# One sum-and-transpose step for four modulation blocks in a four-layer diffusion trunk

## The chip, the cores and the metric

One core of a Trainium2 chip runs the whole program in one launch. The metric is the device time of that launch in microseconds (us); of the kernel before, three timed runs are shown. The five engines are named as the profile names them: PE is TensorE's matmul side and PEld its weight loads, DVE is VectorE, ACT is ScalarE, POOL is GpSimd, SP issues transfers.

## The reference, cut to what matters

Four layers (mixers HGRN2, neighbourhood attention, S5, HGRN2) work on 256 context and 256 latent tokens of width 1024. Each layer has six modulation vectors for the latents and six for the context, made by one large product of two vectors with a matrix of 1024 x 6144:

```
s_lat, s_ctx = jax.nn.silu(c), jax.nn.silu(c_ctx)
for i in range(DEPTH):
    m_l = jnp.split((s_lat @ w_mod[i] + b_mod[i])[:, None, :], N_MOD, axis=-1)
    m_c = jnp.split((s_ctx @ w_mod[i] + b_mod[i])[None, None, :], N_MOD, axis=-1)
    h_l = rmsnorm(lat, norm_g[i, 0]) * (1.0 + m_l[1]) + m_l[0]
    h_c = rmsnorm(cx, norm_g[i, 0]) * (1.0 + m_c[1]) + m_c[0]
    ...
    lat = lat + m_l[2] * rmsnorm(y_l, norm_g[i, 1])
    h_l = rmsnorm(lat, norm_g[i, 2]) * (1.0 + m_l[4]) + m_l[3]
    lat = lat + m_l[5] * rmsnorm(conv_ffn(h_l, ...), norm_g[i, 3])
```

The context stream does the same with `m_c`. The change touches only how `s @ w_mod` is formed and brought into place.

## The kernel before, in words

Activations lie with features on the partitions and tokens along the row. Every large product is done as three single-pass products (high part by high part, low by high, high by low: lines 691 to 693), over 8 slices of the feature axis; ACT and POOL or DVE split the weights into high and low parts (lines 112 and 115) one weight tile ahead. The order of the work is the order in which the program text issues it: each engine runs its instructions in that order, and generators that are advanced at "ticks" put small work between the products. The program runs a mixer and a feed-forward part (FFN) for each layer in turn: HGRN2, FFN, attention, FFN, S5, FFN, HGRN2, FFN.

**Modulation blocks.** `w_mod` is cut into 96 blocks, one for each layer `l`, vector `s` (6) and quarter `b` (4): 1024 rows by 256 columns. `mod_load` (line 293) brings one in by two transfers; there is room for one block ahead after the start. Blocks are formed at slots (`mod_slot`, line 406), which `mod_plan` spreads over a mixer or FFN; `mod_until` forms what is still missing before its use. After the start, the slots hold 12 blocks in the first HGRN2, 12 in FFN 0, 12 in attention, 18 in FFN 1, 6 in S5, 15 in FFN 2, 9 in the last HGRN2 and 4 in FFN 3.

**A block on TensorE** (`mod_block`, line 303) is eight matmuls (line 317), each of a 32-column weight tile `sT` (column 0 the context vector, column 1 the latent one, the other 30 zero) against 256 columns of the block, four of them side by side in four column strips of 32. The PSUM tile `ps` then holds four partial sums for each of the two vectors, in rows 32j and 32j+1. ACT copies it to `mev` in SBUF (line 320, one buffer).

**The sum-and-transpose step** (`mod_flush`, line 372) is issued at the next slot: two matmuls (line 386) with a 128x128 half of `mev` as weights and `sel` (128x2, a one in row 32j+c of column c) as the moving side add the four partial sums and turn the 256 features onto the partitions. DVE adds the bias (`mT`, line 390) and, for four of the six vectors, forms the gain `g` (line 398 or 400).

**A block on VectorE** (`mod_vec`, line 328, in FFN 2 alone: `VO = (2,)`) is 16 DVE instructions on 128x256 (lines 336 and 338), one of them after each slice of a product (`vstep`, called from `mm3`); its step is four one-column matmuls (line 383). In FFN 2, 14 blocks are formed so; the 15th is formed on TensorE just before.

Every fp32 matmul of lines 317, 383 and 386 leaves two records in the trace, so a block shows 16 records, a step 4 (line 386) or 8 (line 383).

Of the kernel before, what the change touches and what calls it, by code (L numbers as in the profile page):

```python
# [6 lines left out]
F32 = mybir.dt.float32  # L7
# [8 lines left out]
NK = 8  # L16
# [39 lines left out]
VK = 1  # L56
VO = (2,)
VG = 8
VR = 1
# [13 lines left out]
VEC = {}  # L73
# [81 lines left out]
class Kern:  # L155
    def __init__(self, tc, ctx, a):
# [8 lines left out]
        self.bg = self.vm = None  # L165
        self.von = False
# [87 lines left out]
    def consts(self):  # L254
# [6 lines left out]
        self.sel = cp.tile([128, 2], F32, name="sel")  # L261
# [41 lines left out]
    def mod_block(self):  # L303
# [22 lines left out]
    def mod_vec(self):
        nc = self.nc
        i = self.mod_nd
        r = self.mod_raw[i]
        acc = self.vpool.tile([128, 2, 256], F32, name="mac", bufs=1)  # L330
        for k in range(NK):
            for v in range(2):
                c = self.sT[:, k, v:v + 1]
                w = r[k // 4][:, k % 4]
                if k == 0:
                    nc.vector.tensor_scalar(acc[:, v], w, c, None, op0=MUL)
                else:
                    nc.vector.scalar_tensor_tensor(acc[:, v], w, c, acc[:, v], op0=MUL, op1=ADD)
                if k == 7 and v == 1:
                    self.mod_raw.pop(i)  # L340
                    self.mod_nd += 1
                    self.mod_load()
                    self.mod_flush()
                    self.mod_pend = (i, acc)
                yield
        for _ in range(VG):
            yield
        self.mod_flush()
        for _ in range(VG):
            yield  # L350

    def mod_finish(self):
        g, self.vm = self.vm, None
        for _ in g:
            pass

    def vstep(self):
        if self.vm is None:
            if not self.von:
                return  # L360
            m = self.mod_sched
            if self.mod_nd >= min(m[0] + m[1], self.mod_end):
                return
            self.vm = self.mod_vec()
        for _ in range(VR):
            try:
                next(self.vm)
            except StopIteration:
                self.vm = None
                return  # L370

    def mod_flush(self):
# [5 lines left out]
        l, s, b = self.mod_order[i]  # L378
        ps = self.aux()
        if len(ev.shape) == 3:  # L380
            for c in range(2):
                for v in range(2):
                    nc.tensor.matmul(ps[:, 2 * c + v:2 * c + v + 1], ev[:, v, c * 128:(c + 1) * 128], self.ones,
                                     start=(c == 0 and v == 0), stop=(c == 1 and v == 1), skip_group_check=True)
# [1548 lines left out]
```

## Time and profile before

| what | value |
|---|---|
| timed runs | 2994.34, 2995.45, 2996.59 us (median 2995.45) |
| the profiled execution: span from first to last instruction | 3001.2 us |
| a time of its own for the profiled execution | none is given beside its span |
| busy, share of the span | PE 92%, PEld 76%, DVE 67%, ACT 43%, POOL 27% |
| records | 53651 |
| mean granted TensorE clock | 0.960 of 2.4 GHz |

The span of the profiled execution is 5.75 us (0.2%) above the median of the timed runs. The page of the profile gives the busy time of each engine, the chain of work that ended last, and groups of instructions by line with mean duration, idle time before them and what ended it; the timeline gives instructions in order of time with start and duration, merged where they repeat. A matmul's duration includes its way through the array, so that the cost of one in a stream is read from the distance between two starts.

### The profile page before, as it was taken

The numbers are of one execution on the slowest core, as the hardware profiler recorded it, in microseconds if no ns is written. First come the engines' busy times: TensorE is split into PE (matmuls) and PEld (weight loads), VectorE is DVE, ScalarE is ACT, GpSimd is POOL, SyncE is SP. The second block draws the span as 40 slices with busy tenths as digits, with TensorE's granted clock in tenths as the row PEclk, the third lists the DMA queues.
The fourth block names the chain that finished last, engine by engine and source line by source line (L and its number), as shares of the span: only waits on it lengthen the run. The fifth ranks groups of instructions, "written<-read, shape, count | busy, mean of one in ns | idle before, by whom it ended". The sixth has DMA issues, their size and how long they took to land.

```text
span 3001.2 us, 53651 instructions
## 1 busy us (share of the span) xinstructions
PE 2769.3 (92%) x21814; PEld 2283.6 (76%) x21814; DVE 2016.9 (67%) x3979; ACT 1285.0 (43%) x2154; POOL 824.1 (27%) x440
## 2 busy tenths in 40 slices
PE   8999997999999999889999876989999888998998
PEld 5777776877788777777778734878888887776998
DVE  5676767776657555687555675378677777776776
ACT  4333333633344544553333565453333453332644
POOL 1111112243324111234332311332221342222443
PEclk9999998999999999999999988999999989998998
DMA  6222321255424342235553388323433442232543
GB/s 248 91 100 85 114 86 71 94 186 187 160 105 144 113 162 106 102 128 192 198 197 140 129 238 255 139 87 139 147 133 138 153 171 102 99 113 89 186 173 116
DMA packets 127046, 421.28 MB, mean 140 GB/s; under 512 B 36048, under 2 KB 55760, under 8 KB 102096
## 3 DMA queue, kind: packets, MB, share of 16 engines
q1 hardware_dynamic: 118608, 391.64, 37.5%
q0 software_dynamic: 5472, 23.07, 2.2%
q8 instruction: 172, 2.82, 0.4%
q10 hardware_dynamic: 2720, 3.15, 0.3%
q14 instruction: 74, 0.61, 0.1%
HBM read 392.78 MB, written 29.23 MB: 141 GB/s over the span
## 4 chain that ended last, share of the span: by engine, by line
PE 65%; DVE 20%; ACT 6%; issue 4%; DMA 3%; SPq 1%; POOL 1%; DVEq 0%; ACTq 0%; POOLq 0%
PE acc L691 16%; PE acc L692 15%; PE acc L693 15%; DVE wlo L115 3%; ACT whi L112 2%; PE aux L317 2%; PE aux L1106 2%; DVE FB L1077 2%; PE acc L727 1%; PE acc L729 1%; PE acc L728 1%; DVE y L564 1%; DVE u L896 1%; DVE P L1047 1%; PE aux L1146 1%
## 5 line engine op out<-in xcount | busy, mean ns | idle before, releaser
L115 POOL TENSOR_TENSOR wlo<-wraw,whi 128x1024 fp32r<-128x1024 f32 (+5 forms) x248 | 627.8, 2532 | 1738.2 <-ACT whi L112 1634.2
L691 PE MATMUL acc<-h,whi 128*128 128x512 f32 (+1 forms) x2368 | 869.7, 367 | 26.8 <-ACT h L577 15.7
L692 PE MATMUL acc<-h,whi 128*128 128x512 f32 (+1 forms) x2368 | 843.2, 356 | 21.1 <-DVE h L584 16.7
L693 PE MATMUL acc<-h,wlo 128*128 128x512 f32 (+1 forms) x2368 | 838.8, 354 | 6.1 <-POOL wlo L115 4.0
L691 PEld LDWEIGHTS acc<-h,whi 128*128 128x128 f32 x2368 | 459.1, 194 | 96.5 <-ACT h L577 18.8
L115 DVE TENSOR_TENSOR wlo<-wraw,whi 128x1024 fp32r<-128x1024 f32 (+5 forms) x248 | 400.5, 1615 | 184.5 <-ACT whi L112 154.5
L692 PEld LDWEIGHTS acc<-h,whi 128*128 128x128 f32 x2368 | 459.7, 194 | 81.4 <-DVE h L584 24.0
L693 PEld LDWEIGHTS acc<-h,wlo 128*128 128x128 f32 x2368 | 459.6, 194 | 67.0 <-POOL wlo L115 4.6
L112 ACT ACTIVATE whi<-wraw 128x1024 fp32r<-128x1024 f32 (+5 forms) x496 | 479.5, 1014 | 68.5 <-PE acc L692 51.2
L691 PE MATMUL acc<-gh,whi 128*128 128x256 f32 (+1 forms) x872 | 297.7, 341 | 11.2 <-ACT gh L897 11.2
L693 PE MATMUL acc<-gh,wlo 128*128 128x256 f32 (+1 forms) x872 | 289.6, 332 | 3.0 <-POOL wlo L115 3.0
L692 PE MATMUL acc<-gl,whi 128*128 128x256 f32 (+1 forms) x872 | 289.7, 332 | 1.0 <-DVE gl L898 0.7
L886 ACT ACTIVATE u<-acc,vec 128x512 f32<-128x512 f32 (+1 forms) x190 | 127.4, 691 | 215.1 <-PE acc L693 214.6
L1077 DVE TENSOR_TENSOR FB<-FB,P 128x256 f32<-128x256 f32 x384 | 165.4, 473 | 37.9 <-PE aux L1106 35.2
L691 PEld LDWEIGHTS acc<-gh,whi 128*128 128x128 f32 x872 | 167.5, 192 | 28.8 <-ACT gh L897 12.0
L889 DVE SCALAR_TENSOR_TENSOR u<-acc,vec,u 128x510 f32<-128x510 f32 (+1 forms) x190 | 122.0, 642 | 97.6 <-ACT u L886 97.5
L693 PEld LDWEIGHTS acc<-gh,wlo 128*128 128x128 f32 x872 | 167.0, 192 | 19.9 <-POOL wlo L115 3.8
L692 PEld LDWEIGHTS acc<-gl,whi 128*128 128x128 f32 x872 | 167.2, 192 | 17.7 <-DVE gl L898 2.3
L896 DVE TENSOR_TENSOR u<-u,u 128x512 f32<-128x512 f32 (+1 forms) x95 | 107.5, 1131 | 37.5 <-ACT u L895 34.2
L897 ACT ACTIVATE gh<-u 128x512 fp32r<-128x512 f32 (+1 forms) x95 | 52.3, 551 | 179.6 <-DVE u L896 179.6
L890 DVE SCALAR_TENSOR_TENSOR u<-acc,vec,u 128x510 f32<-128x510 f32 (+1 forms) x190 | 123.1, 648 | 6.7
L1106 PEld LDWEIGHTS aux<-FB 128*32 128x32 f32 (+1 forms) x4416 | 58.4, 114 | 82.0 <-DVE FB L1077 37.4
(299 smaller groups left out, 4328.4 us busy)
## 6 DMA issues: line engine op xcount, KB each, us to landing
wm<-in_w_mod SPq DMA_DIRECT2D x192, 512.0 KB, 5.0
wraw<-in_f_w_in SPq DMA_DIRECT2D x89, 1024.0 KB, 4.8
wraw<-in_fo SPq DMA_DIRECT2D x44, 896.0 KB, 4.5
wraw<-in_a_qz SPq DMA_DIRECT2D x18, 1024.0 KB, 4.9
wraw<-in_a_zg SPq DMA_DIRECT2D x18, 1024.0 KB, 4.9
wraw<-in_fo SPq DMA_DIRECT2D x16, 1024.0 KB, 4.9
wraw<-in_a_v SPq DMA_DIRECT2D x15, 1024.0 KB, 4.9
wraw<-in_c_glu SPq DMA_DIRECT2D x12, 1024.0 KB, 4.8
```

Source lines behind the costliest of these rows:

```text
L112: nc.scalar.activation(hi[:, a:b], r[:, a:b], AF.Copy)
L115: e.tensor_tensor(lo[:, a:b], r[:, a:b], hi[:, a:b].bitcast(F32), op=SUB)
L317: nc.tensor.matmul(ps[32 * j:32 * j + 32, :256], self.sT[:, k, :], r[q][:, j, :], start=(q == 0), stop=(q == 1), tile_position=(0, 32 * j))
L691: nc.tensor.matmul(ps, wh[:, k], hh, start=(first and k == 0), stop=False, **kw)
L692: nc.tensor.matmul(ps, wh[:, k], hl, start=False, stop=False, **kw)
L693: nc.tensor.matmul(ps, wl[:, k], hh, start=False, stop=(last and k == nk - 1), **kw)
L886: nc.scalar.activation(u, ps[c], AF.Identity, scale=w(1), bias=self.vec[:, cb0 + ch:cb0 + ch + 1])
L889: nc.vector.scalar_tensor_tensor(u3[:, :, 1:], p3[:, :, :255], w(0), u3[:, :, 1:], op0=MUL, op1=ADD)
L890: nc.vector.scalar_tensor_tensor(u3[:, :, :255], p3[:, :, 1:], w(2), u3[:, :, :255], op0=MUL, op1=ADD)
L896: nc.vector.tensor_tensor(us[1], us[0], us[1], op=MUL)
L1077: nc.vector.tensor_tensor(o, o, p, op=MUL)
L1106: nc.tensor.matmul(o, FB[:, d, 1 - d, c:c + w], r, start=True, stop=True, tile_position=(0, w * q))
```

## The change

Blocks 8 to 95 are taken in groups of four quarters `b` = 0 to 3 of one vector. `sT` has 40 columns, with the two vectors in columns 6 and 7, and a block of quarter `b` takes the 32 columns from 6-2b on: its sums then come out in rows 32j+2b and 32j+2b+1, and the other rows are zero. For b = 0 ACT copies PSUM to `mev` (two buffers now); for b = 1, 2, 3 DVE adds PSUM to `mev` in SBUF. Only after b = 3 there is a step: two matmuls with `sel` of 8 columns, two DVE instructions for `mT` (one for each 128-row half, of 4x2 elements) and one for `g` on 16 elements. The first 8 blocks keep a step each. The VectorE form (`mod_vec`, `vstep`, `mod_finish`, lines 336, 338 and 383) is gone, and FFN 2 forms its blocks at slots as the other FFNs do.

```diff
-VO = (2,)
...
-        self.sel = cp.tile([128, 2], F32, name="sel")
+        self.sel = cp.tile([128, 8], F32, name="sel")
...
-        self.sT = cp.tile([128, NK, 32], F32, name="sT")
+        self.sT = cp.tile([128, NK, 40], F32, name="sT")
...
     def mod_block(self):
...
+        b = self.mod_order[i][2] if i >= 8 else 0
...
-                nc.tensor.matmul(ps[32 * j:32 * j + 32, :256], self.sT[:, k, :], r[q][:, j, :],
+                nc.tensor.matmul(ps[32 * j:32 * j + 32, :256], self.sT[:, k, 6 - 2 * b:38 - 2 * b], r[q][:, j, :],
                                  start=(q == 0), stop=(q == 1), tile_position=(0, 32 * j))
-        ev = self.np_.tile([128, 256], F32, name="mev", bufs=1)
-        nc.scalar.activation(ev, ps[:, :256], AF.Copy)
+        if b == 0:
+            ev = self.np_.tile([128, 256], F32, name="mev", bufs=2)
+            nc.scalar.activation(ev, ps[:, :256], AF.Copy)
+        else:
+            ev = self.mod_ev
+            nc.vector.tensor_tensor(ev, ps[:, :256], ev, op=ADD)
         self.mod_flush()
-        self.mod_pend = (i, ev)
+        self.mod_ev = ev
+        if i < 8 or b == 3:
+            self.mod_pend = (i, ev)
...
     def mod_flush(self):
...
-        for c in range(2 if len(ev.shape) == 2 else 0):
-            nc.tensor.matmul(ps[:, 2 * c:2 * c + 2], ev[:, c * 128:(c + 1) * 128], self.sel, start=(c == 0),
+        w = 2 * nb
+        for c in range(2):
+            nc.tensor.matmul(ps[:, w * c:w * c + w], ev[:, c * 128:(c + 1) * 128], self.sel[:, :w], start=(c == 0),
                              stop=(c == 1), skip_group_check=True)
...
     def mm3(self, ps, w, h, nk, ticks=(), first=True, last=True, shared=False):
...
-            if k % VK == VK - 1:
-                self.vstep()
...
     def ffn(self, l, halves, nxt):
...
-                    if l not in VO:
-                        self.mod_slot()
+                    self.mod_slot()
...
-                        if not last and m % 2 and l not in VO:
+                        if not last and m % 2:
                             self.mod_slot()
```

Counted over the whole program, TensorE has 768 instead of 656 block matmuls, 60 instead of 164 + 56 matmuls of steps, DVE 66 adds to `mev` instead of 224 instructions on `mac`, 60 instead of 96 for `mT` and 19 instead of 64 for `g`, ACT 30 copies to `mev` instead of 82. POOL and SP issue the same instructions; on SP the transfers of `w_mod` stand elsewhere among those of the weights in FFN 2.

Where the instructions stand, first on PE in FFN 1, at the third block of a group, before a product with `w_out`. Before, the block is followed by the step of the block ahead of it:

```order
L1541 MATMUL aux<-ident,W 128x128 x4
L317 MATMUL aux<-wm,sT 32x256 x8
L386 MATMUL aux<-sel,mev 128x2 x2
L691 MATMUL acc<-gh,whi 128x512
L692 MATMUL acc<-gl,whi 128x512
```

And the same place with the change (lines 1487, 310, 643 and 644 are the former 1541, 317, 691 and 692):

```order
L1487 MATMUL aux<-ident,W 128x128 x4
L310 MATMUL aux<-wm,sT 32x256 x8
L643 MATMUL acc<-gh,whi 128x512
L644 MATMUL acc<-gl,whi 128x512
```

The two matmuls of the step are gone from this slot; they stand, with 8 columns, at the first slot of the next group.

Second, DVE in FFN 2. Before, two pairs of products (`u` is the convolution, `gl` the low part of its result):

```order
L400 TENSOR_TENSOR g_98<-mT,vec 128x4
L889 SCALAR_TENSOR_TENSOR u_19358<-acc,vec,u_19358 128x2x255
L890 SCALAR_TENSOR_TENSOR u_19358<-acc,vec,u_19358 128x2x255
L889 SCALAR_TENSOR_TENSOR u_19362<-acc,vec,u_19362 128x2x255
L890 SCALAR_TENSOR_TENSOR u_19362<-acc,vec,u_19362 128x2x255
L336 TENSOR_SCALAR mac<-wm,sT 128x256 x2
L338 SCALAR_TENSOR_TENSOR mac<-wm,sT,mac 128x256 x3
L896 TENSOR_TENSOR u_19362<-u_19358,u_19362 128x512
L898 TENSOR_TENSOR gl<-u_19362,gh 128x512
L115 TENSOR_TENSOR wlo<-wraw,whi 128x1024
L338 SCALAR_TENSOR_TENSOR mac<-wm,sT,mac 128x256 x9
```

And with the change, a little later in the same FFN (lines 839, 840, 846, 848, 111 are the former 889, 890, 896, 898, 115; 317 is now the add):

```order
L111 TENSOR_TENSOR wlo<-wraw,whi 128x1024
L839 SCALAR_TENSOR_TENSOR u_19791<-acc,vec,u_19791 128x2x255
L840 SCALAR_TENSOR_TENSOR u_19791<-acc,vec,u_19791 128x2x255
L839 SCALAR_TENSOR_TENSOR u_19795<-acc,vec,u_19795 128x2x255
L840 SCALAR_TENSOR_TENSOR u_19795<-acc,vec,u_19795 128x2x255
L317 TENSOR_TENSOR mev<-aux,mev 128x256
```

Of the 14 or so `mac` instructions between two convolutions one add is left, behind the convolution.

## Rows read from the trace of the kernel before

**Rows 1.** The page: span, busy time by engine, chain that ended last by engine.

```profile
span 3001.2 us, 53651 instructions
...
PE 2769.3 (92%) x21814; PEld 2283.6 (76%) x21814; DVE 2016.9 (67%) x3979; ACT 1285.0 (43%) x2154; POOL 824.1 (27%) x440
...
PE 65%; DVE 20%; ACT 6%; issue 4%; DMA 3%; SPq 1%; POOL 1%; DVEq 0%; ACTq 0%; POOLq 0%
```

**Rows 2.** Windows by stage: length; busy PE, PEld, DVE, ACT, POOL; clock; DMA share, GB/s.

```profile
64.00:540.00 476.00, 435.97 (x5115) 351.42 (x5116) 332.94 (x742) 162.64 (x284) 93.50 (x43) 0.95 0.27 95
540.00:960.00 420.00, 407.19 (x2516) 333.05 (x2514) 282.30 (x454) 181.18 (x287) 144.18 (x80) 1.00 0.43 149
960.00:1300.00 340.00, 318.44 (x2067) 253.15 (x2068) 206.91 (x431) 170.12 (x363) 71.93 (x46) 0.96 0.33 118
1300.00:1695.00 395.00, 387.94 (x2489) 313.77 (x2487) 245.28 (x386) 156.39 (x248) 133.69 (x74) 1.00 0.51 174
1695.00:2008.00 313.00, 244.47 (x2314) 191.09 (x2318) 193.30 (x678) 173.06 (x275) 70.56 (x58) 0.88 0.56 178
2008.00:2365.00 357.00, 352.58 (x1718) 296.51 (x1711) 269.07 (x452) 134.74 (x189) 83.29 (x38) 0.99 0.38 135
2365.00:2772.00 407.00, 360.44 (x3623) 309.07 (x3622) 295.27 (x549) 166.82 (x280) 118.34 (x55) 0.93 0.34 120
2772.00:3001.00 229.00, 209.85 (x1704) 203.52 (x1702) 160.84 (x216) 114.58 (x191) 101.38 (x40) 0.95 0.44 157
```

**Rows 3.** Groups by line and form: PE's blocks and steps (busy us, mean ns).

```profile
L317 PE MATMUL aux<-wm,sT 128*32 128x256 f32 x1312 | 90.2, 391 | 10.9 <-DMA wm<-in_w_mod 10.8
...
L386 PE MATMUL aux<-sel,mev 128*128 128x2 f32 x328 | 50.3, 258 | 1.8 <-ACT mev L320 1.8
```

**Rows 4.** Timeline of PE, a slot in FFN 1: start, duration.

```profile
1327.97 1.07 PE L317 MATMUL aux<-wm,sT 128*32 128x256 f32 x16
1328.98 0.61 PE L386 MATMUL aux<-sel,mev 128*128 128x2 f32 x4
1329.44 0.48 PE L691 MATMUL acc<-h,whi 128*128 128x512 f32 x1
```

**Rows 5.** Timeline of PE, a slot in FFN 1 with no step.

```profile
1301.87 1.07 PE L317 MATMUL aux<-wm,sT 128*32 128x256 f32 x16
1302.87 0.39 PE L691 MATMUL acc<-h,whi 128*128 128x256 f32 x1
```

**Rows 6.** Timeline of PE in FFN 2: the step of a block on VectorE.

```profile
2063.83 0.95 PE L383 MATMUL aux<-ones,mac 128*128 128x1 f32 x8
2064.64 0.47 PE L691 MATMUL acc<-h,whi 128*128 128x512 f32 x1
```

**Rows 7.** Timeline of PE in FFN 2: the step of the last block on VectorE.

```profile
2345.68 1.58 PE L383 MATMUL aux<-ones,mac 128*128 128x1 f32 x8 [1.87 <-DVE mac L338]
2347.12 0.56 PE L691 MATMUL acc<-gh,whi 128*128 128x256 f32 x1
```

**Rows 8.** Windows: the last pairs of FFN 0, and FFN 2 behind rows 7.

```profile
898.00:910.00 12.00, 11.66 (x73) 10.35 (x72) 6.45 (x10) 4.57 (x7) 1.26 (x1) 1.00 0.21 78
...
2346.00:2354.00 8.00, 7.99 (x42) 7.92 (x42) 3.38 (x8) 4.06 (x6) 3.16 (x2) 0.57 0.56 182
```

**Rows 9.** Groups by line and form: DVE and ACT, priced for the change.

```profile
L338 DVE SCALAR_TENSOR_TENSOR mac<-wm,sT,mac 128x256 f32<-128x256 f32 x196 | 97.0, 560 | 0.0
L336 DVE TENSOR_SCALAR mac<-wm,sT 128x256 f32<-128x256 f32 x28 | 19.8, 746 | 0.0
L983 DVE TENSOR_TENSOR y<-acc,y 128x256 f32<-128x256 f32 x64 | 26.4, 417 | 46.1 <-PE acc L693 46.0
L390 DVE TENSOR_TENSOR mT<-aux,vec 128x4 f32<-128x4 f32 x96 | 15.0, 156 | 77.0 <-PE aux L386 61.5 <-PE aux L383 15.4
...
L320 ACT ACTIVATE mev<-aux 128x256 f32<-128x256 f32 x82 | 31.4, 382 | 105.6 <-PE aux L386 99.3 <-PE aux L317 6.2
```

**Rows 10.** Waits of DVE: us in total, times, longest us.

```profile
DVE mT L390 <- PE aux L386: 61.5, 30, 7.3
```

More of the change, by code (lines that the diff above doesn't have):

```diff
@@ L55 @@
 HL = 2
-VK = 1
-VO = (2,)
-VG = 8
-VR = 1
 VX = (0,6,3)
@@ L164, in __init__ @@
         self.dram = pool("dram", space=bass.MemoryType.DRAM)
-        self.bg = self.vm = None
-        self.von = False
+        self.bg = None
         self.gens, self.soft = [], []
@@ L274, in consts @@
         self.g1 = cp.tile([128, 4, 4, NK, 2], F32, name="g1")
-        self.sT = cp.tile([128, NK, 32], F32, name="sT")
+        self.sT = cp.tile([128, NK, 40], F32, name="sT")
         nc.vector.memset(self.sT, 0.0)
-        nc.scalar.activation(self.sT[:, :, 0:2], self.cc.rearrange("p (k i) -> p k i", i=2), AF.Silu)
+        nc.scalar.activation(self.sT[:, :, 6:8], self.cc.rearrange("p (k i) -> p k i", i=2), AF.Silu)
     def mod_setup(self, pool, bufs, first, n):
@@ L307, in mod_block @@
             return
-        if self.vm is not None:
-            self.mod_finish()
-            return
         i = self.mod_nd
         r = self.mod_raw.pop(i)
+        b = self.mod_order[i][2] if i >= 8 else 0
         ps = self.aux()
@@ L321, in mod_block @@
         self.mod_flush()
-        self.mod_pend = (i, ev)
+        self.mod_ev = ev
+        if i < 8 or b == 3:
+            self.mod_pend = (i, ev)
         self.mod_nd += 1
         self.mod_load()
[L326 to L370, printed above, removed]
@@ L378, in mod_flush @@
         l, s, b = self.mod_order[i]
+        b0, nb = (b, 1) if i < 8 else (0, 4)
         ps = self.aux()
[L380 to L384, printed above, removed]
-        for c in range(2 if len(ev.shape) == 2 else 0):
-            nc.tensor.matmul(ps[:, 2 * c:2 * c + 2], ev[:, c * 128:(c + 1) * 128], self.sel, start=(c == 0),
-                             stop=(c == 1), skip_group_check=True)
-        o = VEC["bmod"][0] + l * 48 + s * 8 + b * 2
-        mT = self.mT[:, l, s, 2 * b:2 * b + 2]
-        nc.vector.tensor_tensor(mT, ps[:, :4].rearrange("p (a b) -> p a b", b=2),
-                                self.vec[:, o:o + 2, None].to_broadcast([128, 2, 2]), op=ADD)
+        w = 2 * nb
+        for c in range(2):
+            nc.tensor.matmul(ps[:, w * c:w * c + w], ev[:, c * 128:(c + 1) * 128], self.sel[:, :w], start=(c == 0),
+                             stop=(c == 1), skip_group_check=True)
+        o = VEC["bmod"][0] + l * 48 + s * 8 + b0 * 2
+        ks = slice(2 * b0, 2 * b0 + 2 * nb)
+        mT = self.mT[:, l, s, ks]
+        for c in range(2):
+            nc.vector.tensor_tensor(mT[:, c::2], ps[:, w * c:w * c + w].rearrange("p (b v) -> p b v", v=2),
+                                    self.vec[:, o + c:o + 2 * nb:2, None].to_broadcast([128, nb, 2]), op=ADD)
         n = {1: 0, 2: 1, 4: 2, 5: 3}.get(s)
         if n is not None:
-            o = VEC["ng"][0] + l * 32 + n * 8 + b * 2
-            g = self.vec[:, o:o + 2, None].to_broadcast([128, 2, 2])
-            g1 = self.g1[:, l, n, 2 * b:2 * b + 2]
+            o = VEC["ng"][0] + l * 32 + n * 8 + b0 * 2
+            g = self.vec[:, o:o + 2 * nb, None].to_broadcast([128, 2 * nb, 2])
+            g1 = self.g1[:, l, n, ks]
             if n in (0, 2):
@@ L935, in ffn @@
                 t0 = j0 + nj - (tail if p == len(FSPLIT) - 1 else 0)
-                self.von, self.vpool = l in VO, fp
                 for j in range(n0, t0):
-                    if l not in VO:
-                        self.mod_slot()
+                    self.mod_slot()
                     pair(j, allh, G, (3, 7))
                 last = p == len(FSPLIT) - 1
-                if last:
-                    self.von = False
                 self.cols = last and nxt is None
@@ L1906, in _layout @@
                           1).astype(np.uint32)
-    sel = np.zeros((128, 2), np.float32)
+    sel = np.zeros((128, 8), np.float32)
     for j in range(4):
-        for c in range(2):
+        for c in range(8):
             sel[32 * j + c, c] = 1.0
```

## The prediction

> **What bounds the kernel now.** Start with the page: TensorE is busy for 92% of the span and makes up 65% of the chain that ended last, VectorE 20%, ScalarE 6% [rows 1]. So time taken from TensorE is likely to count, and time put on VectorE counts in part. The windows by stage say where [rows 2]. In order they are the first HGRN2, FFN 0, attention, FFN 1, S5, FFN 2, the last HGRN2, FFN 3. PE is busy for 436.0 of 476 us (92%), 407.2 of 420 (97%), 318.4 of 340 (94%), 387.9 of 395 (98%), 244.5 of 313 (78%), 352.6 of 357 (99%), 360.4 of 407 (89%) and 209.9 of 229 (92%). The FFNs are TensorE's almost alone; in the mixers TensorE and VectorE take turns. In FFN 2 VectorE is busy for 269.1 of 357 us (75%), and still PE is at 99%: the work on VectorE there is covered.
>
> In the groups, blocks on PE are 1312 records (82 blocks of 16) and steps 328 (82 of 4) [rows 3]. Durations overlap, so the cost is read from distances between starts. In a slot of FFN 1 the block takes 1328.98 - 1327.97 = 1.01 us, then the step 1329.44 - 1328.98 = 0.46 us until the next product starts [rows 4]; in a slot without a step the product follows 1.00 us behind the block [rows 5]. The step thus costs PE its full 0.46 us, nearly half a block, for four narrow matmuls' records.
>
> **The change part by part.**
>
> *Steps outside FFN 2.* Blocks 8 to 95 had a step each, 73 of them outside FFN 2, and now 19 are left there: by stage the steps fall from 12 to 3, 12 to 3, 12 to 3, 17 to 4, 7 to 2, (FFN 2), 9 to 3 and 4 to 1. That is 9, 9, 9, 13, 5, 6 and 3 fewer, 54 in all. A step of 8 columns loads the same 128x128 weights, so I take 0.46 us for it too. TensorE saves 54 x 0.46 = 24.8 us. What part is on the path I take from PE's busy share of each stage: 9 x 0.92 + 9 x 0.97 + 9 x 0.94 + 13 x 0.98 + 5 x 0.78 + 6 x 0.89 + 3 x 0.92 = 50.2 steps, 23.1 us. Bounds: 24.8 if all counts; 25 x 0.46 = 11.5 if only FFN 0, 1 and 3 count (9 + 13 + 3).
>
> *FFN 2.* Added are 14 blocks on PE, 14 x 1.00 = 14.0 us, and its steps on PE from `mev` go from 1 to 3, 2 x 0.46 = 0.9. Removed are 14 steps of the VectorE form: 13 x 0.81 (2064.64 - 2063.83) [rows 6] and the last one 2347.12 - 2345.68 = 1.44, together 12.0, and before the last one PE sat idle for 1.87 us until `mac` was ready [rows 7]. Sum: 14.0 + 0.9 - 12.0 - 1.9 = +1.0 us. Behind that idle time the granted clock averages 0.57 over the 8 us from 2346 to 2354, that is, part of them at 1.2 GHz instead of 2.4; at the corresponding place of FFN 0, with no `mac` in VectorE's queue, it is 1.00 [rows 8]. If the stretch goes too, 8 x 0.43 = 3.4 us come back. PE also waits a little for the last pair's `gl` there, in both FFNs, so I count half, 1.7. FFN 2: -0.7, between +2.9 (idle time and clock stay) and -2.4.
>
> *VectorE.* In FFN 2 it loses 97.0 + 19.8 = 116.8 us of `mac` [rows 9]. That buys no time by itself, PE being at 99%. Outside FFN 2 it gains 55 adds. The trace has no add of PSUM to SBUF for `mev`, but the same shape and kinds of operand for `y` on line 983: 417 ns; the other bound is the 560 ns of `mac`, with both inputs in SBUF [rows 9]. I take 417, being the same operation: 22.9 us. Against it, 73 `mT` become 38 and about 49 `g` become 12, at 0.156 each [rows 9]: -5.5 and -5.8. Net +11.6 us, of which 30 of the 55 adds, so 6.3 us, are in the mixers. The FFNs cover the rest (VectorE is busy for 62 to 70% there). In the mixers I put half on the path, 3.2; bounds 0 and 6.3.
>
> The Trainium skill, page "SBUF — State Buffer", section "SBUF: two separate sides", says that a VectorE instruction with two SBUF inputs and a GpSimd one that reads SBUF take an exclusive lock on a shared port, and one blocks the other. The trace agrees as far as it goes: `mac` averages 560 ns, the one-PSUM-input add 417. By that rule the adds keep 417; without it, at 560, they would cost 55 x 0.143 = 7.9 us more of VectorE.
>
> *Waits.* VectorE now waits for the block before each add. It is not a new wait: in the same slots `mT` waited for PE's step, 61.5 us over 30 times [rows 10], and the block ends 0.46 us earlier than that step. Behind the add in the queue stand the convolution's result or the scores' products, as behind `mT`. ScalarE loses 52 copies, 52 x 0.382 = 19.9 us, and most of the 99.3 us it waited behind the step with one buffer [rows 9]. With 43% busy and 6% of the chain I count 0. Each add holds a PSUM buffer as the copy did, and 52 step buffers fewer are taken. On SP the transfers of FFN 2's blocks now wait for PE instead of VectorE; slots are a pair of products apart, so 0.
>
> *Sum.* -23.1 - 0.7 + 3.2 = -20.6 us against the profiled span of 3001.2 us. The median of the timed runs is 5.75 us (0.2%) less than that span, nothing to scale by; the same difference from 2995.45 gives **2975 us**, 0.7% faster. About 0.2%, 6 us, is what a measurement can tell from no change here.
>
> **The rivals.**
>
> *Only the FFNs count* (chance 0.12). In the mixers PE would fill the 0.46 us with waiting for something else, and the added VectorE time would all be on the path. For it: VectorE's 20% of the chain, and that HGRN2 stages leave PE idle for 8 to 11%. Against: those slots lie in runs of products that follow each other without a gap. -11.5 + 1.0 + 6.3 = -4.2, **2991 us**.
>
> *Everything counts, and clock stretches go too* (0.17). All 54 steps, FFN 2 at -2.4, adds hidden: -27.2, **2968 us**. The stages at 0.93 to 0.96 of the clock hold further stretches at 1.2 GHz; two or three of these avoided, at 1.7 us for each 3.4 us of half clock, would bring 2963.
>
> *VectorE becomes the bound* (0.05, slower). An add is late because VectorE is behind, PSUM buffers run out, and PE stands at the next block; the saved 0.46 us is then spent waiting. It decides from the point where VectorE's backlog at a slot exceeds the products ahead of the fourth `aux` buffer. Then the net VectorE time outside FFN 2 is all on the path, nothing is saved, and FFN 2 keeps its +2.9: +14.5, **3010 us**. For it: 67% busy, and that the work goes from the emptier engine to the fuller one. Against: at 11.6 us over 55 slots it is 0.2 us each, less than the 0.46 that PE gives back; and VectorE waited for PE at 30 of these slots, so it was ahead, not behind [rows 10].
> The Trainium skill, page "Perfetto Trace Analysis", section "Optimizing Scalar/DVE Operations", speaks against the change in the same sense: access to PSUM costs VectorE about 125 ns an instruction and ScalarE about 51, and a saturated VectorE should hand work to ScalarE. The rows show 417 against 382 ns [rows 9], a smaller difference, and a VectorE that is not saturated.
>
> That the change does less than it says is excluded by the issue order: 60 matmuls of steps stand there where 220 stood.
>
> **How the numbers follow.** Forecast 0.63 (about 2970 to 2983), everything counts 0.17, only the FFNs 0.12, VectorE bound 0.05, and 0.03 for new clock stretches in the mixers, a dozen at 1.7 us, that take the gain back: no change. Range: the lower end takes in the full saving with some clock stretches, 2965; the upper end goes to just short of the FFN-only case, 2990. Outside are half of the FFN-only case, the slower one and a tail below, some 0.17. Faster by over 0.2%: 0.63 + 0.17 and half of the FFN-only case, 0.86; within 0.2%: the other half and the clock case, 0.09; slower: 0.05.
>
> **What would show it right or wrong.** In the profile after: 1536 block records and 120 of steps; at b = 1, 2, 3 the product follows 1.0 us behind the block's start; 66 adds at 0.41 to 0.43 us. FFN 1's stretch shortens by about 6 us, FFN 0's and attention's by about 4 each, the HGRN2s' by 2 to 4; FFN 2 stays within 3 us of its 357, and PE's idle 1.87 us before its last products are gone. Wrong would be: adds at 0.5 us or more, a wait of PE for `mev` or for an `aux` buffer that an add holds, new stretches at 1.2 GHz in the HGRN2s, or FFNs that do not shorten.

## The result and the profile after

| kernel | median (range, runs) | ratio to before, 95% interval |
|---|---|---|
| before, same comparison | 2996.02 us (2994.34 to 2998.49, 4) | |
| changed | 2981.15 us (2977.50 to 2984.46, 4) | 0.9944 [0.9932, 0.9956] |

The change makes the kernel 0.56% faster: 14.9 us between the medians, where 20.6 was forecast. Two repeats below give 0.9917 and 0.9940; the forecast is a ratio of 0.9932. The profiled execution took 2984.46 us, the slowest of its four; its span is 18.5 us shorter than that of before [rows 1].

The page of the changed kernel: span, busy time, and the chain that ended last by engine.

```profile
span 2982.7 us, 53170 instructions
...
PE 2751.6 (92%) x21718; PEld 2251.8 (75%) x21718; DVE 1939.7 (65%) x3740; ACT 1268.7 (43%) x2102; POOL 823.0 (28%) x440
...
PE 65%; DVE 19%; ACT 6%; DMA 4%; issue 4%; SPq 1%; POOL 1%; ACTq 0%; DVEq 0%; POOLq 0%
```

PE is busy for 17.7 us less than in [rows 1], nearly all of the 18.5. VectorE loses 77 us and falls from 67 to 65%: FFN 2's `mac` weighed more than all the adds. The chain is divided as before.

The windows by stage, in the order and with the columns of [rows 2]; the bounds follow the stages, so that they stand up to 19 us earlier.

```profile
63.00:534.30 471.30, 429.65 (x5079) 345.64 (x5080) 334.55 (x739) 159.04 (x275) 93.21 (x44) 0.96 0.27 96
534.30:950.10 415.80, 403.49 (x2480) 329.37 (x2478) 282.91 (x451) 178.37 (x277) 143.59 (x80) 0.99 0.45 151
950.10:1289.40 339.30, 317.46 (x2030) 249.21 (x2031) 209.37 (x428) 167.37 (x354) 71.92 (x46) 0.95 0.33 118
1289.40:1680.30 390.90, 384.35 (x2437) 309.76 (x2435) 249.69 (x380) 152.14 (x235) 133.13 (x74) 1.00 0.51 176
1680.30:1995.60 315.30, 244.69 (x2294) 191.62 (x2298) 193.13 (x678) 171.93 (x271) 70.55 (x58) 0.87 0.57 177
1995.60:2352.80 357.20, 354.62 (x1838) 286.72 (x1831) 182.63 (x221) 136.43 (x192) 82.44 (x38) 1.00 0.39 135
2352.80:2752.90 400.10, 355.51 (x3598) 306.26 (x3597) 295.06 (x550) 164.45 (x273) 118.72 (x55) 0.94 0.35 122
```

FFN 0 and FFN 1 hold 3.7 and 3.6 us less PE work and are 4.2 and 4.1 us shorter. FFN 2 keeps its 357 us with 86 us less on VectorE. The last HGRN2 is 6.9 us shorter. Attention loses 0.7 us and S5 grows by 2.3, though PE's busy time there is the same to 0.2 us.

The groups by line and form, as [rows 3] and [rows 9]; the first line is the blocks, the second the new adds, the third the merged steps, the fourth what is left of ScalarE's copies.

```profile
L310 PE MATMUL aux<-wm,sT 128*32 128x256 f32 x1536 | 107.5, 394 | 13.9 <-DMA wm<-in_w_mod 13.9
...
L317 DVE TENSOR_TENSOR mev<-aux,mev 128x256 f32<-128x256 f32 x66 | 27.6, 419 | 65.5 <-PE aux L310 65.1
...
L336 PE MATMUL aux<-sel,mev 128*128 128x8 f32 x88 | 13.5, 262 | 0.5 <-DVE mev L317 0.5
...
L314 ACT ACTIVATE mev<-aux 128x256 f32<-128x256 f32 x30 | 11.4, 381 | 39.1 <-PE aux L310 39.1
```

The counts are the forecast ones: 1536 block records, 66 adds at 419 ns, and 120 step records (88 with 8 columns, 32 with 2). The step waited for an add once, for 0.5 us.

The timeline of PE in FFN 2: a slot without a step, and one with the merged step.

```profile
2056.36 0.39 PE L645 MATMUL acc<-h,wlo 128*128 128x512 f32 x1
2056.67 1.07 PE L310 MATMUL aux<-wm,sT 128*32 128x256 f32 x16
2057.67 0.51 PE L643 MATMUL acc<-h,whi 128*128 128x512 f32 x1
2058.01 0.40 PE L644 MATMUL acc<-h,whi 128*128 128x512 f32 x1
...
2068.82 1.07 PE L310 MATMUL aux<-wm,sT 128*32 128x256 f32 x16
2069.82 0.61 PE L336 MATMUL aux<-sel,mev 128*128 128x8 f32 x4
2070.29 0.48 PE L643 MATMUL acc<-h,whi 128*128 128x512 f32 x1
```

The product follows 1.00 us behind the block's start, and the step with 8 columns costs 0.47 us (2070.29 - 2069.82), where the one with 2 columns cost 0.46 [rows 4]. But the product ahead of the block starts 0.31 us before it and the second product behind comes 0.34 us after the first, where products in a row stand 0.23 us apart. From 2056.36 to 2058.01 pass 1.65 us instead of 0.46: inserted between products a block costs 1.19 us, not 1.00.

To place the gain, the starts of the same PE products in two traces were paired; every product of before has its partner. e10's trace has no row: that execution took 3883.1 us, against 2969.3 to 2977.28 us for the other four, and is left out of e10's figures. The change of each stage in us against the first trace of before:

| trace | start | HGRN2 | FFN 0 | attention | FFN 1 | S5 | FFN 2 | last HGRN2 | FFN 3 |
|---|---|---|---|---|---|---|---|---|---|
| changed | -1.0 | -4.7 | -4.2 | -0.7 | -4.1 | +2.3 | +0.2 | -6.9 | +0.6 |
| changed, e2 | -1.0 | -7.4 | -4.4 | -2.8 | -6.2 | -1.0 | -0.5 | -9.1 | +0.9 |
| changed, e9 | -1.9 | -4.7 | -3.9 | -0.7 | -4.8 | +2.7 | -0.4 | -9.3 | +0.7 |
| before, e1 | +0.2 | -0.8 | +0.2 | 0.0 | -0.5 | -0.5 | -2.0 | -3.3 | +3.6 |
| e4 | -1.6 | -0.4 | -0.3 | +1.7 | -1.2 | -1.8 | +6.4 | -1.4 | +3.0 |
| e11 | +0.5 | -0.1 | 0.0 | +0.1 | -0.3 | -2.6 | -5.8 | -4.8 | +0.6 |
| e3 | -1.5 | -4.2 | -3.8 | -0.6 | -4.0 | +1.8 | -2.2 | -7.9 | +0.9 |
| e5 | +0.6 | -3.9 | -3.2 | -1.2 | -6.9 | +4.4 | -0.4 | -9.0 | +0.7 |
| e6 | -2.4 | -2.4 | -0.2 | +2.0 | -2.1 | -1.0 | +6.5 | -5.5 | 0.0 |
| e7 | -0.6 | -4.1 | -5.3 | +2.7 | -6.2 | -1.6 | +0.1 | -9.4 | +0.4 |
| e8 | -0.2 | -3.3 | -4.2 | -2.3 | -6.4 | +0.3 | -5.8 | -10.3 | -1.2 |
| e12 | -1.1 | -5.9 | -4.5 | +3.3 | -7.8 | -1.9 | -4.4 | -9.9 | -1.4 |

Rows of one and the same program differ by up to 2.1 us in FFNs 0 to 2 and by up to 2 to 4 in the mixers and FFN 3, so a single trace does not settle what a mixer gained. The three traces of the changed kernel are therefore compared below with those of the ungrouped kernels: before, e1, e4 and e11, without e4 and e11 in FFN 2, which they change.

The same pairing shows single steps where the stages are too noisy. Taken were 49 slots outside FFN 2 that held a step before and hold none with the change; the distance is that from two products ahead of the slot to four behind it. In the first trace of the changed kernel it is 0.41 to 0.47 us shorter than before at 43 of the 49: 6 of 6 in the first HGRN2, 8 of 9 in FFN 0, 8 of 8 in attention, 11 of 13 in FFN 1, 3 of 5 in S5, 5 of 5 in the last HGRN2 and 2 of 3 in FFN 3.

### The profile page after: what moved, and what is told of

Same layout as the page of the kernel before. It is cut to its first block, busy times and chain, and to the rows that moved or that the text cites. A ratio compares the mean times of both kernels' runs of the same rounds, so it can differ in the third digit from the quotient of the medians.

```text
span 2982.7 us, 53170 instructions
## 1 busy us (share of the span) xinstructions
PE 2751.6 (92%) x21718; PEld 2251.8 (75%) x21718; DVE 1939.7 (65%) x3740; ACT 1268.7 (43%) x2102; POOL 823.0 (28%) x440
## 4 chain that ended last, share of the span: by engine, by line
PE 65%; DVE 19%; ACT 6%; DMA 4%; issue 4%; SPq 1%; POOL 1%; ACTq 0%; DVEq 0%; POOLq 0%
PE acc L643 17%; PE acc L644 16%; PE acc L645 15%; DVE wlo L111 3%; ACT whi L108 3%; PE aux L310 2%; PE aux L1052 2%; DVE FB L1023 2%; PE acc L677 1%; DVE y L516 1%; PE acc L679 1%; PE acc L678 1%; PE aux L1092 1%; DVE bc L417 1%; DVE P L993 1%
## 5 line engine op out<-in xcount | busy, mean ns | idle before, releaser
L644 PE MATMUL acc<-h,whi 128*128 128x512 f32 (+1 forms) x2368 | 846.0, 357 | 21.3 <-DVE h L536 16.8
L643 PEld LDWEIGHTS acc<-gh,whi 128*128 128x128 f32 x872 | 166.8, 191 | 33.5 <-ACT gh L847 12.8
L846 DVE TENSOR_TENSOR u<-u,u 128x512 f32<-128x512 f32 (+1 forms) x95 | 118.7, 1249 | 44.3 <-ACT u L845 41.5
L310 PE MATMUL aux<-wm,sT 128*32 128x256 f32 x1536 | 107.5, 394 | 13.9 <-DMA wm<-in_w_mod 13.9
```

Source lines behind the costliest of these rows:

```text
L643: nc.tensor.matmul(ps, wh[:, k], hh, start=(first and k == 0), stop=False, **kw)
L644: nc.tensor.matmul(ps, wh[:, k], hl, start=False, stop=False, **kw)
L846: nc.vector.tensor_tensor(us[1], us[0], us[1], op=MUL)
```

## The experiments

The theory at this point: the gain comes from the steps that no longer stand between products; FFN 2 comes out even because 14 more blocks on PE pay for 14 steps and one idle time; the adds are hidden or nearly so. The rivals: the gain (or a part) comes from VectorE, which is rid of `mac`; the adds give back what is missing from 20.6; or what is missing is a spread between executions. In the expectations theory A is this theory, with what differs from the forecast left to a TensorE clock that falls differently from execution to execution; theory B, in e1, e2 and e5, is that VectorE's adds are on the path in the mixers. e1 to e4, e5 to e8 and e9 to e12 were each measured as one series together with the kernel before, and medians and ratios are taken within a series.

**e1 and e2: before and the changed kernel again**, with no edit.

> The kernel before, unchanged, to see how much two profiled executions of one program differ by stage. Theory A (the change's gains are as worked out, and what differs from them in attention, FFN 1 and S5 is TensorE clock that falls differently from execution to execution): the time stays at 2996 us, but single stages differ from the first trace of before by 2 to 4 us, together with 3.4 us steps of their time at 1.2 GHz; FFN 0, FFN 1 and FFN 2, hardly ever at 1.2 GHz, agree within 1 us. Theory B (the missing gain in attention and S5 is VectorE time that the adds put on the path): two executions of before agree within 1 us in every stage.

> The changed kernel, unchanged. Both theories: 2981 us, 0.994 to 0.996 of before. Theory A: the stages attention (shorter by 0.7 us in the first trace of after), S5 (longer by 2.3) and the last HGRN2 (shorter by 6.9) come out differently, the first two shorter by some 4 and 1 where they hold no more time at 1.2 GHz than in before; FFN 0 stays at -4.2. Theory B: they come out as in the first trace, within 1 us.

Before against itself gave 0.9994 [0.9985, 1.0003], the changed kernel 0.9917 [0.9904, 0.9931] (median 2977.86 us), which is below the 0.994 to 0.996 that both theories expected. e1's stages differ by up to 3.6 us, as theory A has it and B has not, but FFN 2 by 2.0, more than A allowed. e2's attention and S5 came out shorter than in the first trace, as under A. The first two ratios of the changed kernel, 0.9944 and 0.9917, have intervals that do not overlap; a comparison leaves a spread of about 0.25% that its own interval does not contain. By the granted clock, the first trace of the changed kernel spent 245 us at 1.2 GHz in all and that of e2 207 us, with the same program. The windows of attention, S5 and the last HGRN2 in e2:

```profile
947.20:1284.40 337.20, 315.61 (x2030) 248.43 (x2031) 209.13 (x428) 167.42 (x354) 71.97 (x46) 0.96 0.34 119
...
1673.20:1985.20 312.00, 238.55 (x2294) 188.46 (x2298) 195.12 (x681) 171.97 (x271) 70.71 (x59) 0.90 0.56 179
...
2341.80:2739.60 397.80, 353.35 (x3598) 303.22 (x3598) 295.03 (x550) 164.45 (x273) 118.38 (x55) 0.95 0.35 123
```

S5 with the same 2294 PE instructions holds 6.1 us less of PE's busy time at a clock of 0.90 instead of 0.87, and is 3.3 us shorter; the other two stand one hundredth higher and are 2.1 and 2.3 us shorter.

The record has the mean granted clock of nearly every execution. A fit to the 123 executions that have one (a level for each program, one slope for all, the 3883.1 us one left out) makes an execution 1.06 us longer (standard error 0.13) for each 0.001 of mean clock that it lacks: the execution's clock accounts for part of the spread. At equal clock it puts the changed kernel 20.5 us (0.7) below before. It is a fit and not an experiment, and where an edit itself moves the clock, that part is taken out with it.

**e3: only the grouping.** Before, with the columns, the adds and the merged step of the change; FFN 2 keeps its blocks on VectorE, each with a step of its own.

```diff
+        b = 0 if self.single(i) else self.mod_order[i][2]
...
+            nc.vector.tensor_tensor(ev, ps[:, :256], ev, op=ADD)
...
+    def single(self, i):
+        l, s, _ = self.mod_order[i]
+        return i < 8 or (l, s) in ((2, 5), (3, 1), (3, 0), (3, 2))
```

> Only the grouping: four blocks share a step, with the adds on VectorE, everywhere except for the blocks of FFN 2, which keep the VectorE form and a step each. Outside FFN 2 it issues 54 steps fewer, as the change does, and 54 adds. Theory A: nearly all of the change's gain, 23 us of TensorE less some clock: 2980 us, within 2 us of the changed kernel, FFN 2 as in before (wait of 1.87 us and the clock stretch behind it included). A rival, that the gain comes from emptying VectorE in FFN 2: 2994 us or more.

0.9916 [0.9903, 0.9930], 2976.08 us; the changed kernel in the same series has 0.9917. The grouping alone is worth the whole gain, as expected (within 2 us of the changed kernel). What the change does to FFN 2 is worth nothing that these runs can tell.

**e4: only FFN 2 without VectorE's blocks**, each block with its own step.

```diff
-VO = (2,)
+VO = ()
```

> Only the other part: FFN 2 forms its blocks on TensorE as the other FFNs do, with a step for each block, and no grouping anywhere. From the traces: 14 blocks at 1.09 us and 14 steps at 0.46 added, 13 x 0.81 and 1.44 + 1.87 us removed, and 3.4 us back if the stretch at 1.2 GHz behind the last block goes: 15.3 + 6.4 - 10.5 - 3.3 - 3.4 = +4.5 us in FFN 2, so 3000 us (theory A). If emptying VectorE by 117 us in FFN 2 is what gains: 2985 us or less.

1.0018 [1.0009, 1.0027], 3006.58 us: slower by 5.4 us by the ratio, where 4.5 were expected. FFN 2 takes the loss (+6.4 in the table), and no other stage gains more than the spread from a VectorE rid of 117 us of `mac`. In FFN 2's window of e4 VectorE's busy time is 177.67 us, against 269.07 in [rows 2], and PE's is 8.2 us higher:

```profile
2004.40:2367.70 363.30, 360.75 (x1881) 292.93 (x1874) 177.67 (x226) 140.27 (x203) 82.34 (x38) 1.00 0.39 133
```

That the gain comes from VectorE falls with this run.

**e5: every add twice.** The second goes to a tile that nothing reads, on the same engine and ahead of the slot's next work.

```diff
             nc.vector.tensor_tensor(ev, ps[:, :256], ev, op=ADD)
+            t = self.np_.tile([128, 256], F32, name="mex", bufs=1)
+            nc.vector.tensor_tensor(t, ps[:, :256], ev, op=ADD)
```

> The changed kernel with each of the 66 adds followed by a second one of the same operands into a tile that nobody reads: 66 x 0.417 = 27.5 us more on VectorE, 12.5 us of it in the mixers. Price of the adds as predicted (half of those in the mixers on the path): +6 us over the changed kernel, 0.995 of before. Theory A (they are hidden): +0 to +3 us, 0.992 to 0.994. Theory B (VectorE decides in the mixers): +12 us or more, 0.996 or more.

0.9947 [0.9935, 0.9960], 2982.49 us. The groups of DVE in e5:

```profile
L319 DVE TENSOR_TENSOR mex<-aux,mev 128x256 f32<-128x256 f32 x66 | 28.0, 425 | 2.3
...
L317 DVE TENSOR_TENSOR mev<-aux,mev 128x256 f32<-128x256 f32 x66 | 27.6, 419 | 62.3 <-PE aux L310 61.9
```

28.0 us more on VectorE, some 30 x 0.425 = 12.8 of them in the mixers, put the ratio just above the three of the unedited kernel (0.9917 to 0.9944) and 0.0013 or 4 us above their mean, which is less than these three differ by. That is the value expected if half of the mixers' adds are on the path (0.995), and not in theory A's range (0.992 to 0.994), whose upper end the interval takes in. The fit by the clock puts e5 4.5 us (1.2) above the changed kernel. Paired product by product, attention's stretch from 1010 to 1210 us becomes shorter by 0.4 to 0.5 us at each of its six removed steps, with the add doubled as without: there the adds cost nothing. So some of the doubled adds' time probably reaches the end, in places that the traces do not show; 28 us on the path are excluded.

**e6: the steps put back.** In the changed kernel, two matmuls of the removed step's shape at each slot with b = 1, 2 or 3; their result is not used.

```diff
         self.mod_flush()
+        if b:
+            pd = self.aux()
+            for c in range(2):
+                nc.tensor.matmul(pd[:, 2 * c:2 * c + 2], self.ident, self.sel[:, :2], start=(c == 0),
+                                 stop=(c == 1), skip_group_check=True)
```

> The changed kernel with two matmuls as in a step (128x128 weights, two columns, the identity as weights, the result unused) put back at each of the 66 slots with b = 1, 2, 3, so that the slots cost TensorE what they did before. Theory A (a step's 0.46 us counts by TensorE's share of each stage): 62 of 66 x 0.46 = +28 us over the changed kernel, 1.001 to 1.003 of before, with FFN 0, FFN 1 and FFN 2 longer by 4, 6 and 5 us. If only the FFNs count: 36 x 0.46 = +17 us, 0.998.

1.0007 [0.9998, 1.0016], 3000.51 us. The gain is gone. Of the 49 slots paired above, 43 stand within 0.03 us of before again. Against the mean of the changed kernel's three ratios, 0.9934, that is 0.0073, 22 us for 66 steps or 0.33 us each on average. A slot of FFN 1 in e6, PE's timeline:

```profile
1324.30 1.07 PE L310 MATMUL aux<-wm,sT 128*32 128x256 f32 x16
1325.30 0.61 PE L322 MATMUL aux<-sel,ident 128*128 128x2 f32 x4
1325.76 0.48 PE L648 MATMUL acc<-h,whi 128*128 128x512 f32 x1
```

Each costs 0.46 us where it stands. The sum is 8 us smaller than 66 x 0.46 = 30.4, and the ratio lies just below the 1.001 to 1.003 expected; the changed kernel's own ratios differ by 8 us, so it is not shown whether some of the steps' time does not reach the end. Against the mean of the changed kernel's traces FFN 0, FFN 1 and FFN 2 are longer by 4.0, 2.9 and 6.7 us, where 4, 6 and 5 were expected.

**e7: the sum in PSUM instead.** The four blocks of a group add up in one PSUM tile that is held from b = 0 to 3, ScalarE copies it once, and no add is left; `aux` has three buffers instead of four to make room.

```diff
-        return self.pp.tile([128, 512], F32, name="aux", bufs=4)
+        return self.pp.tile([128, 512], F32, name="aux", bufs=3)
...
+        if b == 0:
+            self.mod_ps = self.pp.tile([128, 512], F32, name="mod", bufs=1)
+        ps = self.mod_ps
...
-                                 start=(q == 0), stop=(q == 1), tile_position=(0, 32 * j))
+                                 start=(q == 0 and b == 0), stop=(q == 1 and (one or b == 3)),
+                                 tile_position=(0, 32 * j), skip_group_check=True)
```

> The changed kernel, but the four blocks of a group are summed by TensorE in one PSUM tile that is held from the first block to the copy behind the fourth, instead of by adds on VectorE. The tile takes one of the four aux buffers, so the other users have three. Theory A (adds hidden, four buffers not all needed): within 3 us of the changed kernel, 0.992. If the adds cost what was predicted: 3 us better. If the fourth buffer carries the HGRN2s and attention: slower than the changed kernel by 10 us or more, in these stages, with TensorE waiting for copy_predicated or for ScalarE's evacuations.

0.9933 [0.9921, 0.9946], 2978.81 us, within the spread of the changed kernel: in sum, taking the adds away buys nothing that these runs can tell. But the edit has a price of its own. Paired, PE loses 1.3 us at 1035 us and 1.2 at 1144, both in attention; of the runs with fewer steps only e7 and e12 have an attention that is not shorter. At both places PE's score products wait for ScalarE's `P`, and in that stretch the changed kernel has no such wait. And PE waits for the held tile. The waits from 1000 to 1150 us, and in the whole program (us in total, times, longest):

```profile
PE aux L1199 <- ACT P L1205: 0.6, 2, 0.3
...
PE mod L313 <- ACT mev L319: 3.3, 3, 1.6
```

**e8: VectorE's blocks kept, and ended earlier.** e3 showed PE waiting for `mac` at the end of FFN 2 as before did, and behind that wait slower products. PE's timeline there, e3:

```profile
2330.52 0.28 PE L708 MATMUL acc<-gh,wlo 128*128 128x256 f32 x1
2332.64 1.23 PE L394 MATMUL aux<-ones,mac 128*128 128x1 f32 x8 [1.85 <-DVE mac L349]
2333.73 0.37 PE L706 MATMUL acc<-gh,whi 128*128 128x256 f32 x1
...
2334.30 0.41 PE L707 MATMUL acc<-gl,whi 128*128 128x256 f32 x1
2334.51 0.41 PE L708 MATMUL acc<-gh,wlo 128*128 128x256 f32 x1
```

Products stand 0.21 us apart at the end, and 0.12 before the wait; the granted clock averages 0.79 from 2332 to 2340 us, so part of it is at 1.2 GHz. e8 is e3, and begins no VectorE block in the last two pairs of FFN 2:

```diff
                 for j in range(n0, t0):
+                    if p == len(FSPLIT) - 1 and j >= t0 - 2:
+                        self.von = False
```

> The run with grouping only, and FFN 2 begins no VectorE block in its last two pairs of products, so that no step waits for mac at its end: 13 instead of 14 blocks in the VectorE form, the other one moves to the last HGRN2 on TensorE. Expected in FFN 2 against before: 0.81 + 1.44 - 0.81 + 1.87 = 3.3 us less and up to 3.4 us of clock; in the last HGRN2 1.09 + 0.47 = 1.6 us more. In all 2 to 4 us below the run with grouping only, 0.990 to 0.991 of before.

0.9911 [0.9897, 0.9924], 2971.72 us (2970.36 to 2972.38), the lowest median so far, though its ratio is only 0.0005 (1.5 us) below e3's, where 2 to 4 us were expected. FFN 2's window in e8 takes 351.2 us where it took 354.8 in e3 and 357 in before, and a window over its last products holds the full clock (2.4 GHz):

```profile
1991.90:2343.10 351.20, 348.64 (x1710) 292.54 (x1703) 263.80 (x448) 134.34 (x189) 83.80 (x38) 1.00 0.39 134
...
2324.00:2332.00 8.00, 6.87 (x53) 6.26 (x52) 4.45 (x7) 5.04 (x8) 3.16 (x2) 1.00 0.25 77
```

**e9 and e10: the changed kernel and e8 again**, with no edit.

> The changed kernel once more, in the same call as the runs it is compared with: 0.992 to 0.994 of before, and by stage FFN 0 at -4, FFN 1 at -4 to -6, FFN 2 within 1 us of before. Theory A: attention, S5 and the HGRN2s again differ from the two earlier traces of the same program by 2 to 4 us.

> The run with grouping and the shorter tail of FFN 2 once more: FFN 2 at -5 to -6 us against before, as in its first trace, the rest as in the changed kernel; 0.990 to 0.9915 of before, 4 to 6 us below the changed kernel in the same call.

The changed kernel: 0.9940 [0.9928, 0.9953], 2980.40 us. e8: 0.9914 [0.9900, 0.9928], 2972.26 us. Within this series e8 is 8.1 us below the changed kernel, where 4 to 6 were expected. In e9's trace FFN 0, FFN 1 and FFN 2 come out as expected (-3.9, -4.8, -0.4), but theory A's 2 to 4 us only in part: the first HGRN2, attention and S5 are within 0.4 us of the first trace, and 2 to 4 us from e2's.

**e11: only the earlier end, in the kernel before.** The edit is the one of e8.

> The kernel before, with FFN 2 beginning no VectorE block in its last two pairs, and nothing grouped. If the 1.87 us wait for mac, its slow step and the clock behind it are what FFN 2 gave back in the changed kernel: FFN 2 at -3.3 us and up to -3.4 more, the last HGRN2 at +1.6, so 0.9983 to 0.9995 of before. If the wait only makes room for the next one (the product that follows waits for its weights anyway): 1.000.

0.9969 [0.9957, 0.9981], 2989.78 us: 8.2 us below before in the same series, a larger gain than the 0.9983 to 0.9995 expected. The stage table puts it in FFN 2 (-5.8, against 0 and -2.0 for the two traces of before; -3.3 and up to -3.4 more were expected). The -2.6 of S5, which the edit does not touch, lies in the spread. The last HGRN2 has -4.8, although it holds 10 blocks on PE instead of 9 and was expected 1.6 us longer; before's second trace has -3.3 there.

**e12: e8 with the sum in PSUM**, the edits of e7 and e8 together on e3.

> Grouping with the sum in PSUM (three aux buffers), FFN 2 with VectorE blocks and the shorter tail: no adds on VectorE at all. If the adds cost the changed kernel what was predicted, 3 us below the run with grouping and shorter tail, 0.989 to 0.990 of before; theory A (adds hidden, and attention loses with three buffers): equal to it within 2 us.

0.9911 [0.9896, 0.9926], 2970.09 us. Not to be told apart from e8 and e10, as theory A expected. In attention its trace has +3.3, as e7's has +2.7; both have three `aux` buffers and the same two short waits for `P`.

**The best version** is e8 (or e12): grouping outside FFN 2, VectorE's blocks kept in it and ended two pairs earlier. It is at 0.9911 and 0.9914 of before, and 8.1 us below the changed kernel in the series that holds both; in the traces its FFN 2 is 5.6 us shorter than the mean of the changed kernel's three.

## Why the prediction was right, and where its terms were off

The direction, the size and the mechanism hold. Forecast were -20.6 us; the three comparisons of the changed kernel give -0.56%, -0.83% and -0.60% of 2995.45, that is -16.8, -24.9 and -18.0 us, mean -19.9. The mean stage changes of its three traces against the ungrouped ones sum to -20.7. That the sum is met so closely is luck: the three comparisons differ by 8 us, more than the 6 us that the prediction took as what a measurement can tell, and the stages miss their terms by up to about 4 us in both directions. What is shown is the price of a step and where it counts. By its steps:

| step of the prediction | forecast, us | mean of the traces, us |
|---|---|---|
| first HGRN2: 9 steps, adds | -3.8, and its part of +3.2 | -5.3 |
| FFN 0: 9 steps | -4.0 | -4.1 |
| attention: 9 steps, adds | -3.9, and its part | -1.9 |
| FFN 1: 13 steps | -5.9 | -4.5 |
| S5: 5 steps, adds | -1.8, and its part | +2.5 |
| FFN 2 | -0.7 | +0.8 |
| last HGRN2: 6 steps, adds | -2.5, and its part | -6.0 |
| FFN 3: 3 steps | -1.3 | -1.1 |
| start | 0 | -1.1 |

**The steps outside FFN 2: right.** The price of 0.46 us holds, with 8 columns too (0.47). e3 has the whole gain by the grouping, and e6 loses it with the steps put back. Within a run of products a removed step returns 0.41 to 0.47 us, in the mixers as in the FFNs (43 of 49 slots, above), and e6 takes it back at as many. Forecasting a stage by PE's busy share was right in the sum and rough in the parts: what the rows of one program differ by from trace to trace is as large as the term of a mixer.

**FFN 2: right in kind, about 1.5 us off in the sum.** The mis-sized terms are the 14 blocks, priced at 1.00 us from the block's own start, and the 14 VectorE steps, priced at 0.81 in the same way. Between products a block costs 1.19 (above). For the step the timeline of PE in before, around [rows 6], has

```profile
2063.60 0.40 PE L693 MATMUL acc<-h,wlo 128*128 128x512 f32 x1
...
2064.95 0.39 PE L692 MATMUL acc<-h,whi 128*128 128x512 f32 x1
```

that is 1.35 us instead of 0.46, or 0.89. So a slot loses 1.19 - 0.89 = 0.30 us and not 0.19, over 14 slots 1.5 us more. That equals what the sum is off by; but the waits at FFN 2's end (below) and the share of the clock that the prediction halved are as large, and no run takes them apart. The 1.87 us of idle time and the stretch at 0.57 of the clock [rows 7, 8] are gone, as said. Before, PE had waited there for `gh` and `gl` as well:

```profile
2341.52 0.38 PE L691 MATMUL acc<-gh,whi 128*128 128x256 f32 x1 [0.75 <-ACT gh L897]
...
2342.24 0.39 PE L692 MATMUL acc<-gl,whi 128*128 128x256 f32 x1 [0.34 <-DVE gl L898]
```

What is late next is small: PE's timeline at FFN 2's end in the changed kernel

```profile
2334.68 0.39 PE L643 MATMUL acc<-gh,whi 128*128 128x256 f32 x1 [0.30 <-ACT gh L847]
...
2335.41 0.39 PE L644 MATMUL acc<-gl,whi 128*128 128x256 f32 x1 [0.34 <-DVE gl L848]
...
2337.71 0.39 PE L645 MATMUL acc<-gh,wlo 128*128 128x256 f32 x1 [0.51 <-POOL wlo L111]
```

with 1.15 us of waits in place of 0.75 + 0.34 + 1.87 = 2.96, and windows that hold the full clock (2.4 GHz):

```profile
2336.00:2344.00 8.00, 7.50 (x63) 7.26 (x62) 5.80 (x6) 4.54 (x8) 5.01 (x3) 1.00 0.33 116
```

**VectorE's +3.2 us: the price right, the share on the path not settled.** An add takes 419 ns, forecast 417. "In the mixers I put half on the path" fails where it can be seen product by product: at attention's slots doubled adds cost nothing. For the whole kernel e5 (+4 us by the ratios, 4.5 by the fit) allows anything from none, given the spread, to half (6.4 us for 12.8 doubled), and e7, with no adds, is not clearly faster (1.3 us (1.1) by the fit) but pays for its lost buffer. The other bound, `mac`'s 560 ns, was a mean over unlike things; the tile's view of before gives shortest, median and longest:

```profile
L338 DVE SCALAR_TENSOR_TENSOR mac<-wm,sT,mac x196: 467/476/2626, 2027.5 to 2345.5; 128x256 f32<-128x256 f32 x196
```

The same view of the adds in the changed kernel:

```profile
L317 DVE TENSOR_TENSOR mev<-aux,mev x66: 409/417/427, 135.1 to 2835.8; 128x256 f32<-128x256 f32 x66
```

The adds, with one input from PSUM, were never stretched; `mac`, with both from SBUF, was, to over five times its median. That agrees with the rule of the Trainium skill, page "SBUF — State Buffer", section "SBUF: two separate sides", on the port that two SBUF inputs lock. The trace of before shows GpSimd as the other side: each of the 10 instructions of line 338 over 600 ns (and of the 7 of line 336) starts while GpSimd splits a weight tile and ends 0.15 to 0.29 us after it does. One of them:

```profile
2150.97 2.40 POOL L115 TENSOR_TENSOR wlo<-wraw,whi 128x1024 fp32r<-128x1024 f32 x1 [8.71 <-ACT whi L112]
2151.43 2.23 DVE L338 SCALAR_TENSOR_TENSOR mac<-wm,sT,mac 128x256 f32<-128x256 f32 x1
```

Of the 66 adds in the changed kernel 25 start during a GpSimd instruction, and all 66 take 409 to 427 ns.

**The waits: right at 0.** PE's step waited for an add once, 0.5 us. VectorE's wait at the slots, 61.5 us at 30 places [rows 10], is 65.1 us at 17 now, and behind it nothing is late:

```profile
DVE mev L317 <- PE aux L310: 65.1, 17, 8.3
```

**The rivals.** Only the FFNs count: refuted by the single steps in the mixers, where 22 of 24 slots return 0.41 to 0.47 us, by e6 (1.0007, where this rival gave 0.998), and by the first and the last HGRN2, which gained 5.3 and 6.0 us. Everything counts and clock stretches go too, 2968 us: e2 comes near it (0.9917 x 2995.45 = 2970.6), with 207 us at 1.2 GHz against 245 in the first trace (before's two have 240 and 228), but the program is the same, so it is no property of the change; the other two ratios give 2978.7 and 2977.5. VectorE as the bound: refuted by e5, where 28 us more of it cost about 4 by the means.

**What stays open.** Attention gained 2.0 us less than its steps and S5 became 2.5 us longer, while the HGRN2s gained 5 us more than their steps. S5's shift is in the first trace, e9, e3 and e5, and not in e2, e6, e7, e8 and e12, and goes with the clock of that stage in the traces of the changed kernel (82 and 85 us at 1.2 GHz in the first and e9, 65 in e2), but not in e5, whose S5 has 68 us and the largest shift; whether the doubled adds are on the path there is not shown. Nor is it shown that the edits set where the clock falls, and not chance alone: the three traces of the changed kernel disagree among themselves.

## What to carry to other kernels

A small step between large products costs by its instructions rather than its columns (0.46 us with 2, 0.47 with 8): four of these steps in one took as long as one did, and collecting them, with the sums on an engine that has room, was the whole gain. Price such an insertion between the products around it (1.19 us here), not from its own start (1.00). Before an engine is relieved, look at what it delays: 117 us of `mac` taken from VectorE bought nothing, while ending its blocks two pairs earlier bought 8.2 us in the kernel before, since the last of them held up PE at the end of a stage; on top of the grouping it bought 3.6 us in FFN 2's window, and 1.5 us by the ratios, which is inside their spread.

## What the runs showed of the hardware

One program, with the same products in the same order, showed spans of 2982.7, 2969.7 and 2978.6 us in its three traces, and 245, 207 and 234 us at 1.2 GHz. The differences lie mostly in the mixers, where PE is idle for longer, and are of the size of the terms to be measured. The runs of one comparison agree better than comparisons of the same kernel do: [0.9932, 0.9956] and [0.9904, 0.9931]. By the fit over the executions, 0.001 of mean clock, 3.0 us of the span, moves the time by 1.06 us.

One execution on the one core, e10's profiled one, ran at a mean granted clock of 0.627; over its first 1000 us the clock averages 0.56 to 0.57, and behind that 0.65. The view of its core (span, mean granted clock) and a line of its page:

```profile
core 0: 3881.3 us, clock 0.627
```

```profile
PE 3765.8 (97%) x21610; PEld 2726.9 (70%) x21610; DVE 2014.7 (52%) x3969; ACT 1276.8 (33%) x2101; POOL 816.2 (21%) x440
```

PE was busy for 97% of it, 3765.8 us where e8's trace of the same program has 2737.3, while VectorE's and ScalarE's busy times are near those of before [rows 1]. What set the clock is not shown.
